# Moving the copies of a bias table from the GpSimd queue to the queue of the weight loads

## The chip, the cores and the metric

The kernel runs on one core of one Trainium2 chip. The metric is the device time of one execution in microseconds (us); lower is better. A core has TensorE (PE, with its weight loads PEld), VectorE (DVE), ScalarE (ACT), GpSimd (POOL) and SyncE (SP). SP computes nothing here: it issues DMAs. DMAs issued from SP, ACT and POOL are listed as separate queues, and the transfers of all queues are carried by the core's 16 DMA engines.

## The reference, cut to what matters

The reference is two transformer-like blocks for one sequence of 256 tokens with 1024 features, all in float32. The first block has two layers, each with a SwiGLU FFN, an attention and a second FFN, all modulated by a conditioning vector; the second block has convolutions, an attention to a memory and a feed-forward part with 16384 experts. The change concerns the attention of the first layer alone, a differential attention with a relative-position bias:

```python
def diff_attention(h, w_qkv, w_o, lam_params, subln_g, rel_bias, lambda_init):
    ...
    lf = lam_params.astype(jnp.float32)
    lam = jnp.exp(jnp.sum(lf[0] * lf[1])) - jnp.exp(jnp.sum(lf[2] * lf[3])) + lambda_init
    table = rel_bias.astype(jnp.float32)
    ...
        rel = q_pos[:, None] - k_pos[None, :]
        bias = jnp.take(table, t5_bucket(rel), axis=0)
        bias = jnp.transpose(bias, (2, 0, 1))[None, :, None]
        logits = jnp.einsum('bqhmd,bkhmd->bhmqk', qb, k).astype(jnp.float32) * scale + bias
        logits = jnp.where(rel >= 0, logits, -jnp.inf)
        p = jax.nn.softmax(logits, axis=-1)
        w = p[:, :, 0] - lam * p[:, :, 1]
        return jnp.einsum('bhqk,bkhe->bqhe', w.astype(v.dtype), v)
    ...
    o = rms_norm(o, subln_g) * (1 - lambda_init)
```

The bias depends on the head (8 of them) and on the distance of query and key alone, so for one head it is one line of values, shifted by one place from query to query.

## The kernel before, in words

Activations lie with features on the partitions: `xT` is 128 partitions x 8 x 256 tokens. Each float32 weight is split into a high and a low part, so that a product takes three matmuls (`mm3`, L147 to L149). Weights come through the class `Weights`: SP loads 1 MB into one of 3 `raw` buffers (L105); a raw tile has two pieces of 128x1024, and each is split by ACT (`whi`, L115) and DVE (`wlo`, L116) into one of 4 pairs of buffers, which TensorE reads. The modulation weights (`araw`, L355) go through SP too, as background work between the weight loads, and are reduced on DVE (L358).

The kernel begins with keys and values of the memory. Then comes `ffn(0, ...)`, the first FFN: 22 output tiles j of the hidden layer (one raw tile each, `ffn_in`), then 8 output tiles n of the projection back (`ffn_out`). For each n, `residual` updates `xT` on DVE, ACT squares the new tile (`sq`, L182, three buffers) and POOL adds the squares up (`sqa`, L193). The sum is multiplied with ones on TensorE (`po`, L177), and from that come the root mean square and the row of scales that the attention needs (`rstd`, L198 and L199; `along_row`, L215; `row`, L243). While the sum is made, TensorE runs the first pair of query tiles on the unscaled activations (`Norm.pair`); then `Norm.scale` writes the scaled `hi` and `lo` (L270 to L275), and the attention goes on. The second FFN ends in the same way, before the keys of the second layer.

The generator `prepare_bias` works beside the first FFN. Its first step loads a one-hot table, the bias table and the lambda parameters. The second multiplies them on TensorE to 8 lines of 384 values (8 partitions, one for each head; `mrow`) and writes these to DRAM (`line`). Then, for each pair of heads q, POOL copies the two lines 128 times to DRAM (`rows`, L515) and reads them back into `TB` (L517) with a step of 383, one less than a row, so that partition p gets its line shifted by p. The last two steps compute lambda (`ls`, L524; the exponent, L528; `nlam`, L529 and L530) and the scale `g08` (L526). The loop over j calls `next(beside)` at j = 4, 6, 8, 10, 12 and 14. `TB` is first read by the heads of the attention (L573).

`TB`, `nlam`, `g08` and the query tiles `qz` lie in the pool `tb`, whose space was used before by other tiles; `const` is a pool that lives from the beginning. The order of instructions on each engine is not that of the source: the framework's scheduler lays it out when the program is built, by its own estimate of when each instruction can start, and the instruction waits on the chip for what it needs. Each engine runs its own instructions in that order.

Of the kernel before, what the change touches and what calls it, by code (L numbers as in the profile page):

```python
# [10 lines left out]
F32 = mybir.dt.float32  # L11
# [42 lines left out]
def forward(ctx: ExitStack, tc: tile.TileContext, io, out, tap=None):  # L54
    nc = tc.nc
    pe, act, dve, pool, sync = nc.tensor, nc.scalar, nc.vector, nc.gpsimd, nc.sync

    const = ctx.enter_context(tc.tile_pool(name="const", bufs=1))
# [8 lines left out]
    def bank(tag, shape):  # L67
        return ps.tile(shape, F32, tag=tag, name=tag, bufs=BANKS[tag])

    def mm_bank(shape):  # L70
        return bank("mm", shape)

    def work(tag, shape, dt=F32, bufs=2, pool_=None):
        return (pool_ or wkp[0]).tile(shape, dt, tag=tag, name=tag, bufs=bufs)
# [13 lines left out]
    def v(name, i=0, n=1):  # L88
        c = VEC[name][0] + i
        return vec[:, c:c + n]  # L90
# [48 lines left out]
    def tick():  # L139
        rate[1] += rate[0]  # L140
        while rate[1] >= 1.0:
            rate[1] -= 1.0
            step()

    def mm3(o, a, b, start, stop):

        pe.matmul(o, a[0], b[0], start=start, stop=False)  # L147
        pe.matmul(o, a[0], b[1], start=False, stop=False)  # L148
        pe.matmul(o, a[1], b[0], start=False, stop=stop)  # L149
# [5 lines left out]
    def blk(piece, k, n=128):  # L155
        return piece[0][:, k * n:(k + 1) * n], piece[1][:, k * n:(k + 1) * n]

    def split_into(pair_hi, pair_lo, src, func=AF.Copy, **kw):

        act.activation(pair_hi, src, func, **kw)  # L160
        dve.tensor_tensor(pair_lo, src, pair_hi, op=ALU.subtract)  # L161
# [115 lines left out]
    def fm_pair(p0, p1, h):  # L277

        o = [mm_bank([128, T]), mm_bank([128, T])]
        for k in range(KT):  # L280
            for oo, pp in zip(o, (p0, p1)):
                mm3(oo, blk(pp, k), tok(h, k), k == 0, k == KT - 1)
        return o

    def fm_one(p, h, h32=None, n=T):
        o = mm_bank([128, n])
        for k in range(KT):
            if len(p) == 1:
                pe.matmul(o, p[0][:, k * 128:(k + 1) * 128], h32[:, k, :], start=(k == 0), stop=(k == KT - 1))  # L289
                continue  # L290
            mm3(o, blk(p, k), tok(h, k, 0, n), k == 0, k == KT - 1)
        return o
# [95 lines left out]
    def mod(name):  # L388
        while name not in mods:
            next(ada)  # L390
        return mods[name]
# [33 lines left out]
    def residual(n, o, s, st, norm):  # L425
        dve.scalar_tensor_tensor(xT[:, n, :], o, s, xT[:, n, :], op0=ALU.mult, op1=ALU.add)
        st.add(xT[:, n, :])
        norm.add(n)


    def ffn(f, norm, gate, following, more=None, done=False):

        with tc.tile_pool(name="ff", bufs=1) as fp:
            ghi = fp.tile([128, FKT, T], F32R, name="ghi")
            glo = fp.tile([128, FKT, T], F32R, name="glo")
            src = io[f"ffn_in{f}"]
            h = norm.h
            for j in range(FKT):
                if f == 0 and j in (4, 6, 8, 10, 12, 14):
                    next(beside)  # L440
                it = W.pieces(src[j])
                if j == 0 and not done:
                    og, ou = norm.pair(next(it), next(it))
                elif j < 2:
                    og, ou = fm_pair(next(it), next(it), h)
                else:
                    og = fm_one(next(it), h)
                    ou = fm_one(next(it), h)
                sg = work("sil", [128, T], bufs=2)
                act.activation(sg, og, AF.Silu)  # L450
                pr = work("pr", [128, T], bufs=2)
                dve.tensor_tensor(pr, sg, ou, op=ALU.mult)
                split_into(ghi[:, j, :], glo[:, j, :], pr)
                tick()
            tc.keep_in_program_order(act.preload_act_table(AF.Sqrt))
            s = mod(gate)
            st = Stat()
            nxt = following()
            src = io[f"ffn_out{f}"]

            def stream():
                for c in range(src.shape[0]):
                    for p in W.pieces(src[c]):
                        for k in range(8):
                            yield blk(p, k)
                    tick()

            wb = stream()
            for n in range(KT):
                o = mm_bank([128, T])  # L470
                for k in range(FKT):
                    mm3(o, next(wb), (ghi[:, k, :], glo[:, k, :]), k == 0, k == FKT - 1)
                residual(n, o, s[:, n:n + 1], st, nxt)
                if more is not None:
                    more.add(xT[:, n, :], scale=v("final_g", n))
        return st, nxt
# [8 lines left out]
    tbp = ask.enter_context(tc.tile_pool(name="tb", bufs=1))  # L485
    dram = ask.enter_context(tc.tile_pool(name="dr", bufs=1, space=bass.MemoryType.DRAM))
    TB = tbp.tile([128, 8, 256], F32, name="TB")
    nlam = tbp.tile([128, 1], F32, name="nlam")
    g08 = tbp.tile([128, 1], F32, name="g08")
    qz = [tbp.tile([128, 2, 256], F32, name=f"qz{i}") for i in range(4)]  # L490
    for t in qz:
        pool.memset(t[64:128, 0, :], 0.0)
# [2 lines left out]
    def prepare_bias():  # L495
        oh = tbp.tile([32, 384], F32, name="oh")
        rb = tbp.tile([32, 8], F32, name="rb")
        lamb = tbp.tile([128, 4, 64], F32, name="lamb")
        la = io["a_lambda"]
        pool.dma_start(out=oh, in_=io["t5"])  # L500
        pool.dma_start(out=rb, in_=io["rel_bias"])
        pool.dma_start(out=lamb, in_=bass.AP(tensor=la.tensor, offset=la.offset, ap=[[0, 128], [64, 4], [1, 64]]))
        mrow = tbp.tile([8, 384], F32, name="mrow")
        pool.memset(mrow[:, 0:256], 0.0)
        pool.memset(mrow[:, 256:384], BIG)
        yield
        pf = bank("lg", [8, 384])
        pe.matmul(pf, rb, oh, start=True, stop=True)
        dve.scalar_tensor_tensor(mrow, pf, -1.0, mrow, op0=ALU.mult, op1=ALU.add)
        line = dram.tile([8, 384], F32, name="line")  # L510
        pool.dma_start(out=line, in_=mrow)
        for q in range(4):
            yield
            rows = dram.tile([2, 128, 384], F32, name=f"rows{q}")
            pool.dma_start(out=rows, in_=line[2 * q:2 * q + 2, :].unsqueeze(1).to_broadcast([2, 128, 384]))  # L515

            pool.dma_start(out=TB[:, 2 * q:2 * q + 2, :],  # L517
                           in_=bass.AP(tensor=rows.tensor, offset=rows.offset + 127,
                                       ap=[[383, 128], [128 * 384, 2], [1, 256]]))
        yield  # L520
        lj = tbp.tile([128, 64], F32, name="lj")
        ls = tbp.tile([128, 2], F32, name="ls")
        for i in range(2):
            dve.tensor_tensor_reduce(out=lj, in0=lamb[:, 2 * i, :], in1=lamb[:, 2 * i + 1, :], scale=1.0,  # L524
                                     scalar=0.0, op0=ALU.mult, op1=ALU.add, accum_out=ls[:, i:i + 1])
        dve.tensor_scalar(g08, v("a_subln_g"), 1.0 - LAM0, None, op0=ALU.mult)  # L526
        yield
        act.activation(ls, ls, AF.Exp)  # L528
        dve.tensor_tensor(nlam, ls[:, 1:2], ls[:, 0:1], op=ALU.subtract)  # L529
        dve.tensor_scalar(nlam, nlam, -LAM0, None, op0=ALU.add)  # L530
        yield

    norm = norm_of("0_sc1", "0_sh1")
    norm.scale(r=st.rstd())
    beside = prepare_bias()
    next(beside)
    st, norm = ffn(0, norm, "0_gt1", lambda: norm_of("0_sc2", "0_sh2"), done=True)
    if tap:
        tap("x_ffn0", xT)
# [105 lines left out]

    rate[0] = 0.56
    st, norm = ffn(1, norm.scaled_by(st), "0_gt3", lambda: norm_of("k_sc1", "k_sh1"))
    rate[0] = 0.4
    if tap:
# [331 lines left out]
    with tc.tile_pool(name="pe0", bufs=1) as p0:  # L981
# [125 lines left out]
        with tc.tile_pool(name="pe1", bufs=1) as p1:  # L1107
# [90 lines left out]
            for t in range(2):  # L1198
# [13 lines left out]
                rows = out[t * 128:(t + 1) * 128]  # L1212
# [102 lines left out]
def program(arrays):  # L1315
    import concourse.bacc as bacc

    nc = bacc.Bacc("TRN2", target_bir_lowering=False, num_devices=1)
    io = {n: nc.dram_tensor(n, a.shape, mybir.dt.from_np(a.dtype), kind="ExternalInput").ap()
          for n, a in arrays.items()}  # L1320
    out = nc.dram_tensor("out", (T, D), F32, kind="ExternalOutput").ap()
    with tile.TileContext(nc) as tc:
        forward(tc, io, out)
    return nc
# [9 lines left out]
```

## Time and profile before

| | |
|---|---|
| median of 3 runs | 2270.47 us (2269.82 to 2273.29) |
| the profiled execution | 2270.32 us, its span 2268.5 us |
| TensorE busy | 98% of the span, mean granted clock 0.996 |
| VectorE, ScalarE, GpSimd busy | 77%, 55%, 4% |
| bytes moved by DMA | 467.76 MB, mean 206 GB/s |

A time such as 260 us is counted from the start of the span. The share of an engine is what it was busy of the span; "x" is followed by a number of instructions. In "A <- B: 7.8, 1, 7.8", the instruction A was held by B for 7.8 us in total, in one place, at most 7.8 us. [...]

### The profile page before, as it was taken

Reading aid. Unit: us, or ns where it says so; the run is one execution under the profiler, and the core shown is the slowest. Engines: PE = TensorE matmul, PEld = TensorE weight load, DVE = VectorE, ACT = ScalarE, POOL = GpSimd, SP = SyncE. Lnnn points to the kernel's source line nnn. Section 1 sums busy time; section 2 is a strip of 40 time slices with the busy share of each in tenths; the row PEclk is TensorE's granted clock in tenths of the full one; section 3 lists DMA queues with packets and bytes.
Section 4 is the critical chain, followed back from the end, with each engine's and each line's share of the span. In section 5 each row is a group of like instructions: output and inputs, shape, how many; then the busy total and the mean of one; then the engine's idle time right before and its main releaser. Section 6 shows DMA issues by size and latency. Waiting matters only on the chain.

```text
span 2268.5 us, 42687 instructions
## 1 busy us (share of the span) xinstructions
PE 2229.0 (98%) x16748; PEld 2131.5 (94%) x16748; DVE 1739.7 (77%) x3501; ACT 1258.6 (55%) x2389; POOL 85.3 (4%) x89
## 2 busy tenths in 40 slices
PE   8999899999999999999999999999999999999998
PEld 8999898999999999999999999999999999888887
DVE  7878667977777787765799886999668997666665
ACT  5544477544654457545523555445567776555555
POOL 0100000000100020000100010000000000000000
PEclk9999899999999999999999999999999999999999
DMA  9887644777668763555444453345543434555554
GB/s 364 297 325 300 231 168 164 301 275 293 245 263 300 292 231 129 216 182 182 164 159 165 161 219 115 117 184 186 186 155 144 145 136 152 193 192 188 185 187 157
DMA packets 68377, 467.76 MB, mean 206 GB/s; under 512 B 9888, under 2 KB 10184, under 8 KB 12368
## 3 DMA queue, kind: packets, MB, share of 16 engines
q1 hardware_dynamic: 64608, 461.67, 54.9%
q0 software_dynamic: 3280, 2.84, 0.5%
q8 instruction: 132, 2.16, 0.4%
q14 instruction: 69, 0.57, 0.1%
q10 hardware_dynamic: 288, 0.52, 0.1%
HBM read 463.88 MB, written 2.63 MB: 206 GB/s over the span
## 4 chain that ended last, share of the span: by engine, by line
PE 92%; DVE 3%; ACT 3%; issue 1%; POOL 0%; DMA 0%; ACTq 0%; DVEq 0%; POOLq 0%
PE mm L149 22%; PE mm L147 22%; PE mm L148 22%; PE mm L1171 8%; PE lg L1171 8%; PE lg L1126 2%; PE mm L289 2%; PE po L177 1%; ACT whi L115 1%; DVE wlo L116 1%; DVE lo L238 0%; DVE lo L275 0%; DVE nt L270 0%; PE po L962 0%; ACT e L576 0%
## 5 line engine op out<-in xcount | busy, mean ns | idle before, releaser
L115 ACT ACTIVATE whi<-raw 128x1024 fp32r<-128x1024 f32 x696 | 733.9, 1059 | 624.2 <-PE mm L148 414.6
L116 DVE TENSOR_TENSOR wlo<-raw,whi 128x1024 fp32r<-128x1024 f32 x696 | 850.5, 1226 | 295.8 <-ACT whi L115 291.0
L147 PE MATMUL mm<-hi,whi 128*128 128x256 f32 x3144 | 900.2, 287 | 2.6 <-ACT hi L274 2.1
L149 PE MATMUL mm<-hi,wlo 128*128 128x256 f32 x3144 | 892.7, 284 | 1.3 <-DVE wlo L116 1.2
L148 PE MATMUL mm<-lo,whi 128*128 128x256 f32 x3144 | 887.2, 282 | 0.1
L147 PEld LDWEIGHTS mm<-hi,whi 128*128 128x128 f32 x3144 | 595.2, 190 | 5.0 <-ACT hi L274 2.6
L149 PEld LDWEIGHTS mm<-hi,wlo 128*128 128x128 f32 x3144 | 596.4, 190 | 3.0 <-DVE wlo L116 2.7
L148 PEld LDWEIGHTS mm<-lo,whi 128*128 128x128 f32 x3144 | 596.9, 190 | 1.8 <-DVE wlo L116 0.6
L149 PE MATMUL mm<-ghi,wlo 128*128 128x256 f32 x704 | 197.4, 280 | 0.0
L147 PE MATMUL mm<-ghi,whi 128*128 128x256 f32 x704 | 197.4, 280 | 0.0
L148 PE MATMUL mm<-glo,whi 128*128 128x256 f32 x704 | 197.4, 280 | 0.0
L358 DVE CUSTOM_DVE_ANT_0 araw<-araw,cb 128x1024 f32<-128x1024 f32 x160 | 191.4, 1225 | 1.0 <-ACT cb L407 1.0
L160 ACT ACTIVATE vph<-S 128x128 fp32r<-128x128 f32 x256 | 77.1, 302 | 131.9 <-PE lg L1171 131.8
L148 PEld LDWEIGHTS mm<-glo,whi 128*128 128x128 f32 x704 | 132.7, 188 | 0.0
L147 PEld LDWEIGHTS mm<-ghi,whi 128*128 128x128 f32 x704 | 132.7, 188 | 0.0
L149 PEld LDWEIGHTS mm<-ghi,wlo 128*128 128x128 f32 x704 | 132.7, 188 | 0.0
L161 DVE TENSOR_TENSOR vpl<-S,vph 128x128 fp32r<-128x128 f32 x256 | 73.4, 288 | 44.3 <-PE lg L1171 43.8
L824 DVE SCALAR_TENSOR_TENSOR cfc<-cf,vec,cfc 128x256 f32<-128x256 f32 x240 | 100.0, 490 | 0.0
L1118 DVE TENSOR_SCALAR ohA<-cst,sel 128x128 f32<-128x128 f32 x256 | 82.2, 342 | 21.8 <-PE lg L1126 20.8
L1171 PE MATMUL mm<-whi,vph 128*128 128x512 f32 x256 | 80.7, 395 | 0.2 <-ACT vph L160 0.2
L1171 PE MATMUL mm<-wlo,vph 128*128 128x512 f32 x256 | 80.9, 395 | 0.0
L1171 PE MATMUL lg<-whi,vpl 128*128 128x512 f32 x256 | 80.8, 395 | 0.0
(392 smaller groups left out, 3277.7 us busy)
## 6 DMA issues: line engine op xcount, KB each, us to landing
raw<-ffn_in SPq DMA_DIRECT2D x88, 1024.0 KB, 4.9
araw<-ada SPq DMA_DIRECT2D x72, 1024.0 KB, 6.9
raw<-peer_u SPq DMA_DIRECT2D x64, 1024.0 KB, 4.8
raw<-peer_v SPq DMA_DIRECT2D x64, 1024.0 KB, 4.8
raw<-ffn_out SPq DMA_DIRECT2D x44, 1024.0 KB, 4.8
araw<-kv_ada SPq DMA_DIRECT2D x8, 1024.0 KB, 6.8
raw<-w_cf SPq DMA_DIRECT2D x8, 1024.0 KB, 4.7
raw<-w_scx SPq DMA_DIRECT2D x8, 1024.0 KB, 4.8
```

Of the source, the lines that this page charges most:

```text
L115: act.activation(hi[:, :m], r, AF.Copy)
L116: last_split[0] = dve.tensor_tensor(lo[:, :m], r, hi[:, :m], op=ALU.subtract)
L147: pe.matmul(o, a[0], b[0], start=start, stop=False)
L148: pe.matmul(o, a[0], b[1], start=False, stop=False)
L149: pe.matmul(o, a[1], b[0], start=False, stop=stop)
L160: act.activation(pair_hi, src, func, **kw)
L161: dve.tensor_tensor(pair_lo, src, pair_hi, op=ALU.subtract)
L289: pe.matmul(o, p[0][:, k * 128:(k + 1) * 128], h32[:, k, :], start=(k == 0), stop=(k == KT - 1))
L358: dve.tensor_tensor_reduce(out=raw[:, i, :], in0=raw[:, i, :], in1=cb, scale=1.0, scalar=0.0, op0=ALU.mult, op1=ALU.add, accum_out=acc[:, ...
L824: dve.scalar_tensor_tensor(o, cf[:, i, j:j + T], w, o, op0=ALU.mult, op1=ALU.add)
L1118: dve.tensor_scalar(A, iota, sel3[:, 0, t:t + 1], sel3[:, 2, t:t + 1], op0=ALU.is_equal, op1=ALU.mult)
L1171: pe.matmul(acc[t][d], lh, rh[:, d * 512:(d + 1) * 512], start=s0, stop=s1)
```

## The change

The copies and read-backs of the bias table are issued by SP, the queue of the weight loads, and no longer by POOL. The DRAM tile `line` is gone: each of the 8 lines is copied from its own partition of `mrow`, 128 times, straight to `rows`, so there are two copies for each pair of heads where there was one. All copies are issued first, one pair of heads a step, and then the four read-backs, one a step. The steps stand at each j from 3 to 12 (ten steps), where they stood at six even j from 4 to 14. `nlam` and `g08` are allocated in the pool `const`.

```diff
             for j in range(FKT):
-                if f == 0 and j in (4, 6, 8, 10, 12, 14):
+                if f == 0 and 3 <= j <= 12:
                     next(beside)
...
-    nlam = tbp.tile([128, 1], F32, name="nlam")
-    g08 = tbp.tile([128, 1], F32, name="g08")
+    nlam = const.tile([128, 1], F32, name="nlam")
+    g08 = const.tile([128, 1], F32, name="g08")
...
         dve.scalar_tensor_tensor(mrow, pf, -1.0, mrow, op0=ALU.mult, op1=ALU.add)
-        line = dram.tile([8, 384], F32, name="line")
-        pool.dma_start(out=line, in_=mrow)
+        copies = []
         for q in range(4):
             yield
             rows = dram.tile([2, 128, 384], F32, name=f"rows{q}")
-            pool.dma_start(out=rows, in_=line[2 * q:2 * q + 2, :].unsqueeze(1).to_broadcast([2, 128, 384]))
-
-            pool.dma_start(out=TB[:, 2 * q:2 * q + 2, :],
+            copies.append(rows)
+            for i in range(2):
+                hd = 2 * q + i
+                sync.dma_start(out=rows[i:i + 1], in_=mrow[hd:hd + 1, :].unsqueeze(1).to_broadcast([1, 128, 384]))
+        for q, rows in enumerate(copies):
+            yield
+
+            sync.dma_start(out=TB[:, 2 * q:2 * q + 2, :],
                            in_=bass.AP(tensor=rows.tensor, offset=rows.offset + 127,
                                        ap=[[383, 128], [128 * 384, 2], [1, 256]]))
         yield
```

## Rows read from the trace of the kernel before

**Rows 1.** The page: busy time by engine, and the chain by engine.
```profile
PE 2229.0 (98%) x16748; PEld 2131.5 (94%) x16748; DVE 1739.7 (77%) x3501; ACT 1258.6 (55%) x2389; POOL 85.3 (4%) x89
...
PE 92%; DVE 3%; ACT 3%; issue 1%; POOL 0%; DMA 0%; ACTq 0%; DVEq 0%; POOLq 0%
```
**Rows 2.** Windows; the columns are named in the first line.
```profile
core 0: us, PE busy (x) PEld busy (x) DVE busy (x) ACT busy (x) POOL busy (x), PEclk, DMA share, GB/s
60.00:70.00 10.00, 9.17 (x70) 8.38 (x68) 6.43 (x17) 5.39 (x10) 2.52 (x9) 1.00 0.51 215
70.00:80.00 10.00, 9.48 (x57) 8.41 (x58) 9.57 (x16) 5.45 (x9) 2.08 (x5) 0.83 0.77 239
150.00:160.00 10.00, 10.00 (x86) 10.00 (x85) 7.12 (x11) 5.27 (x8) 0.00 (x0) 1.00 0.84 316
260.00:300.00 40.00, 29.68 (x214) 28.33 (x213) 24.75 (x43) 18.29 (x35) 5.47 (x4) 0.83 0.39 152
585.00:625.00 40.00, 38.58 (x319) 37.13 (x317) 29.85 (x54) 26.56 (x46) 7.04 (x2) 1.00 0.64 241
```
**Rows 3.** Waits from 260 to 290 us: total us, times, longest.
```profile
POOL sqa L193 <- ACT sq L182: 44.1, 1, 44.1
...
PE po L177 <- POOL sqa L193: 7.8, 1, 7.8
```
**Rows 4.** Timeline of ACT, ends of the first and second FFN: start, duration.
```profile
222.66 0.42 ACT L182 ACTIVATE sq<-xT 128x256 f32<-128x256 f32 x1 [0.21 <-DVE xT L426]
...
265.96 2.00 ACT L115 ACTIVATE whi<-raw 128x1024 fp32r<-128x1024 f32 x2 [3.92 <-issue]
267.87 1.01 ACT L182 ACTIVATE sq<-xT 128x256 f32<-128x256 f32 x3
...
582.92 0.42 ACT L182 ACTIVATE sq<-xT 128x256 f32<-128x256 f32 x1 [0.30 <-DVE xT L426]
...
591.08 0.40 ACT L182 ACTIVATE sq<-xT 128x256 f32<-128x256 f32 x1
```
**Rows 5.** Timeline of POOL in the first FFN.
```profile
125.23 1.09 POOL L515 DMA_DIRECT2D rows<-line  x1
140.24 0.75 POOL L517 DMA_DIRECT2D TB<-rows  x1 [13.92 <-DMA rows<-line]
215.73 1.20 POOL L193 TENSOR_TENSOR sqa<-sq 128x256 f32<-128x256 f32 x1 [74.74 <-ACT sq L182]
216.88 0.74 POOL L517 DMA_DIRECT2D TB<-rows  x1
...
268.42 5.70 POOL L193 TENSOR_TENSOR sqa<-sqa,sq 128x256 f32<-128x256 f32 x4 [44.06 <-ACT sq L182]
```
**Rows 6.** DMA, 85 to 200 us: queues with packets, MB, share; issues with landing.
```profile
q1 hardware_dynamic: 4750, 34.59, 80.2%
q0 software_dynamic: 3088, 2.40, 7.2%
...
rows<-line POOLq DMA_DIRECT2D x4, 384.0 KB, 26.6
TB<-rows POOLq DMA_DIRECT2D x3, 256.0 KB, 14.2
```
**Rows 7.** SP issues kA<-FT (16 KB, one partition written), and a window around it.
```profile
625.75 0.62 SPq L698 DMA_DIRECT2D kA<-FT  x1
...
626.90:627.30 0.40, 0.40 (x5) 0.40 (x4) 0.00 (x0) 0.40 (x3) 0.00 (x0) 1.00 0.17 41
```
**Rows 8.** A raw load on SP, its splits, and landings of raw, 85 to 180 us.
```profile
120.88 0.33 SPq L105 DMA_DIRECT2D raw<-ffn_in  x1
...
132.89 1.06 ACT L115 ACTIVATE whi<-raw 128x1024 fp32r<-128x1024 f32 x1 [1.50 <-issue]
...
135.77 1.06 ACT L115 ACTIVATE whi<-raw 128x1024 fp32r<-128x1024 f32 x1 [1.55 <-PE mm L148]
...
134.88 1.22 DVE L116 TENSOR_TENSOR wlo<-raw,whi 128x1024 fp32r<-128x1024 f32 x1
...
DMA to landing us min/median/max: 4.7/8.1/10.8
```
**Rows 9.** Timeline of DVE: the first use of the table.
```profile
300.26 0.29 DVE L573 CUSTOM_DVE_ANT_0 e<-lg,TB 128x128 f32<-128x128 f32 x1 [0.35 <-PE lg L570]
```
**Rows 10.** Timelines of DVE and ACT around the write of g08.
```profile
67.15 0.16 DVE L526 TENSOR_SCALAR g<-vec 128x1 f32<-128x1 f32 x1 [2.64 <-PE mm L149]
68.06 0.88 DVE L275 SCALAR_TENSOR_TENSOR lo<-nt,mod_sh,hi 128x256 fp32r<-128x256 f32 x2 [0.75 <-ACT hi L274]
...
66.79 0.84 ACT L323 ACTIVATE xa_v<-mm,rstd 128x256 f32<-128x256 f32 x2 [3.68 <-PE mm L149]
```

## The prediction

> **What bounds the kernel now.** I read four views in this order: the page's busy shares and chain, windows around the end of the first FFN beside the end of the second, the waits and the order on ACT and POOL there, and the DMA view of the first FFN.
>
> TensorE bounds the whole: busy 98% of the span, 92% of the chain that ended last [rows 1]. The steps of the change lie in the first FFN and act on the attention that follows it. Inside the FFN TensorE never waits: 10.00 of 10 us, 86 matmuls [rows 2]. So an edit there can only cost, unless it reaches a place where TensorE stands.
>
> There is one such place. At the end of the first FFN, 260 to 300 us, TensorE is busy 29.68 of 40 us and runs 214 matmuls at a mean granted clock of 0.83; the same passage at the end of the second FFN, 585 to 625 us, has 38.58 us, 319 matmuls and clock 1.00 [rows 2]. The longest TensorE wait there is the row statistic's matmul for `sqa` on POOL, 7.8 us; POOL in turn had waited 44.1 us for a square from ACT [rows 3]. The order on ACT says why: the third square runs at 222.66, then the next three come in one block at 267.87, behind two weight splits at 265.96. At the end of the second FFN each square stands beside its own tile (582.92, 591.08) [rows 4]. A square needs one of three buffers, so the fourth waits until POOL has added the first two. On POOL the bias DMAs share that stretch: the read-back of table part 2 at 140.24, the first addition at 215.73, the read-back of part 3 only at 216.88, the last four additions together at 268.42 [rows 5]. The copy that part 3 needs was issued at 125.23 [rows 5] and landings of such copies take 26.6 us [rows 6], so it had been in DRAM since about 152. That it stands behind an addition of 215 us shows an order laid out for a far slower bias chain on POOL. I read the late squares as the consequence: when the order was made, POOL was taken up by DMAs, the additions were late, and the squares lost their buffers.
>
> **The change, part by part.** The base is the profiled execution, 2270.32 us: 1.8 us beside its span of 2268.5 and 0.15 under the median of 2270.47.
>
> *POOL is freed.* One `line` write, four copies and four read-backs leave POOL. If the squares then fall in beside their tiles, this passage costs what the second FFN's does. By matmuls: 40 us at 86 per 10 us are 344; 130 are missing here, 25 there; 105 at 0.116 us are 12.2 us. [...] I take 12.2 us. Above: all 130, 15.1 us. Below: nothing, if the order stays.
>
> *The copies.* Eight copies of 128 rows x 1536 B (196.6 KB) go on SP's queue, each from one partition. Before, a pair was one DMA from a DRAM line. Their data has to pass the same 16 engines, now in one queue with the weight loads, so what counts is how long a copy holds that queue. No row shows a read from a single partition. From below: POOL's queue moved 2.40 MB, copies included, in 7.2% of 115 us [rows 6], 8.3 us of all engines, so 0.7 us a copy. From above: half of a 26.6 us landing, 13.3 us a copy. The nearest row is a transfer of 16.4 KB into one partition: the stretch 626.90 to 627.30 holds it whole, at 0.17 of the engines and 41 GB/s [rows 7]. By its engine time (0.068 us for 16.4 KB) a copy costs 0.8 us, by its elapsed time at most 4.8 us. I take the geometric middle, 2.0 us: 16 us for eight.
>
> What covers it: a raw load issued at 120.88 is split at 132.89, 12.0 us later [rows 8]: the fifth split after it, since two tiles of two pieces lie ahead. A split waits for one of four buffers, so three pieces of 2.88 us lie ahead of TensorE, 8.6 us, less 1.06 and 1.22 us for the split itself [rows 8]: 6.3 us more. Landing takes 4.7 us at least [rows 8], which leaves 13.6 us; loads that landed in 10.8 us stopped nothing. The SP queue fills 80.2% of the engines [rows 6], so four tiles of 5.75 us have 4.6 us to spare. Cover: 18.2 us, or 2.3 us a copy. My 16 us fit; a weight load would be next to be late, then the splits, then TensorE. Cost: 0.
>
> *The read-backs.* Four of 256 KB: by the engine time above about 0.9 us each; their former landing was 14.2 us [rows 6]. SP must wait for the copies four steps earlier, with weight loads queued behind it and TensorE waiting for those. If a step really stands at its output tile, four tiles (23 us) pass in between and there is no wait; if the steps move together, SP holds for one landing under load, 8.1 to 10.8 us [rows 8], inside the 13.6. The bias is first used at 300.26 [rows 9], so the table has over 100 us. Cost: 0. Twelve DMA issues at 0.33 us are 4 us of a queue that mostly waits [rows 8].
>
> *Steps one tile earlier.* The small matmul, its VectorE evacuation and the lambda exponent stay the same instructions. The exponent's two table loads on ScalarE are 2.6 us, covered by a TensorE that is busy throughout; that is my bound for either sign.
>
> *Lambda out of the pool.* VectorE's write of `g08` waits 2.64 us for TensorE, in a pool whose space was in use. But the next VectorE instruction then waits 0.75 us for ScalarE, which itself was held by an earlier evacuation until 66.79 [rows 10]. So the end of this stall goes to ScalarE: gain 0. At most it reorders the start of the FFN: 45 matmuls short of 172 in 60 to 80 us [rows 2], 5.2 us.
>
> Sum: 2270.3 - 12.2 = 2258.1. Own range 2252 (all of 15.1 and part of the 5.2) to 2266.
>
> [...] The kA transfer moved 16.4 KB in 0.4 us [rows 7], at least 41 GB/s on one partition. [...]
>
> **The rivals.**
>
> *A single partition feeds slowly.* A copy takes 4.8 to 8 us and holds the weight queue. For it: 16.4 KB are a twelfth of a copy, and a copy is 128 reads of one row; copies from one DRAM line landed only after 26.6 us. Against: the 41 GB/s. At 6.4 us eight take 51.2 us, less 18.2 of cover: TensorE stands 33 us, in the first FFN. 2258 + 33 = 2291; at 4.8 us 2278, at 8 us 2304, at 13.3 us 2346. It decides against the change from 3.8 us a copy, where (8 x 3.8 - 18.2) eats the 12.2. [...]
>
> *Around that point.* At 3.2 to 4.4 us a copy gain and stall cancel: 2266 to 2275.
>
> *The change doesn't do what frees the passage.* The squares stay late since the order has another cause, for instance that the splits of the value projection were simply ready first. For it: these splits do stand ahead of the squares [rows 4]. Against: the second FFN has the same splits and no such block. With hidden copies: 2270.
>
> **How the numbers follow.** Forecast 0.42: the order on POOL speaks plainly, the copy price is the nearest row's. Slow partition 0.36: its price has no row against it of the same kind. Cancelling 0.09. Order unchanged 0.13, of which 0.11 near 2270 and 0.02 faster through lambda. A measurement of this kernel tells 0.2% (4.5 us) from no change. Faster: 0.42 + 0.02 = 0.44. Same: 0.09 + 0.11 = 0.20. Slower: 0.36. Forecast 2258; the range must reach into the slow case: 2251 to 2303 leaves out copies above 7.9 us (about 0.12) and a little below (0.05).
>
> **What would show it.** Right: squares beside their tiles near 207 to 262, additions on POOL one by one, no wait of `po` for `sqa`, clock 1.00 in 260 to 300, about 320 matmuls there, and raw loads in the FFN landing under 13 us. Wrong: TensorE waiting for splits and splits for raw loads between 85 and 180, with raw landings of 20 us and more (slow partition); or the three squares in a block again after the pair (order unchanged); or SP waiting long for `rows` at the read-backs. The weakest step is the 2.0 us a copy.

## The result and the profile after

The changed kernel takes 2292.02 us (median of 4 runs, 2290.52 to 2293.17) against 2271.38 us for the kernel before on the same chip: ratio 1.009, 95% interval 1.0073 to 1.0108. It is 20.6 us slower, where 12.2 us faster was forecast; the time lies inside the range, at the price of the rival "a single partition feeds slowly". The profiled execution has a span of 2291.4 us.

The page after, busy times and the chain by engine, to be read beside [rows 1]:

```profile
PE 2232.0 (97%) x16748; PEld 2138.6 (93%) x16748; DVE 1740.8 (76%) x3501; ACT 1259.8 (55%) x2389; POOL 76.2 (3%) x80
...
PE 90%; DVE 3%; ACT 3%; DMA 2%; issue 1%; POOL 0%; ACTq 0%; DVEq 0%; POOLq 0%; SPq 0%
```

POOL has nine instructions fewer. New in the chain is DMA with 2%, and the page's chain by line puts 2% to `raw<-ffn_in`: in the changed kernel weight loads set the end for a while. The windows after, in the columns of [rows 2], show where:

```profile
80.00:90.00 10.00, 10.00 (x83) 10.00 (x84) 9.06 (x19) 8.19 (x12) 0.00 (x0) 1.00 0.79 137
90.00:100.00 10.00, 10.00 (x86) 10.00 (x85) 3.52 (x7) 2.15 (x5) 0.00 (x0) 1.00 0.86 29
100.00:110.00 10.00, 0.58 (x5) 0.38 (x4) 0.85 (x2) 0.42 (x1) 0.00 (x0) 0.64 0.86 27
110.00:120.00 10.00, 2.54 (x10) 2.25 (x11) 2.72 (x3) 2.00 (x2) 0.00 (x0) 0.50 0.94 231
120.00:130.00 10.00, 6.17 (x40) 5.96 (x39) 2.78 (x6) 0.80 (x2) 0.00 (x0) 0.84 0.89 87
130.00:140.00 10.00, 5.97 (x26) 5.68 (x27) 4.99 (x8) 2.01 (x2) 0.00 (x0) 0.50 0.94 205
140.00:150.00 10.00, 4.26 (x28) 3.76 (x28) 2.31 (x4) 2.80 (x4) 0.00 (x0) 0.84 0.95 313
...
260.00:300.00 40.00, 40.00 (x341) 40.00 (x340) 30.43 (x38) 18.74 (x24) 5.09 (x5) 1.00 0.71 266
```

The last two columns of the second and third line are the finding: the 16 DMA engines are busy 86% of the time and move 27 to 29 GB/s, where the first FFN before has 316 GB/s at a share of 0.84 [rows 2]. The busy share alone does not say how much data flows. TensorE lives on its buffers until 100 us and then stands, and while it stands its granted clock, the share of full speed at which it was allowed to run, falls to 0.50 (110 to 120 us). The last line is the other half of the story: the passage that had 214 matmuls in 40 us [rows 2] has 341 at clock 1.00. (This FFN ends later than before, so the stretch does not hold the same work; that the end of the FFN itself runs full is shown by the next line of the window, 300 to 340 us with 39.98 us busy and 322 matmuls, and by the squares further down.)

The DMA view after, 84 to 112 us: packets and mean rate, then the queue with packets, MB and share:

```profile
DMA packets 550, 0.80 MB, mean 28 GB/s; under 512 B 50, under 2 KB 547, under 8 KB 547
...
q1 hardware_dynamic: 549, 0.78, 85.7%
```

In 28 us 0.78 MB pass, in packets nearly all of them under 2 KB: four copies of 128 rows. That is 7.0 us a copy for these four (196.6 KB at 28 GB/s). The waits after, 95 to 155 us, and the chain of the stretch (start, us):

```profile
PE mm L147 <- ACT whi L115: 30.5, 6, 16.7
...
ACT whi L115 <- DMA raw<-ffn_in: 24.9, 4, 14.6
```

```profile
96.05 20.12 DMA raw<-ffn_in
116.24 31.13 DMA raw<-ffn_in
```

TensorE waits for splits, the splits for raw loads, and two raw loads take 20 and 31 us of the chain. The prediction had named this as the mark of the slow partition. SP's own timeline says how the loads got behind the copies:

```profile
82.99 12.96 SPq L517 DMA_DIRECT2D rows<-mrow  x4
96.05 7.12 SPq L105 DMA_DIRECT2D raw<-ffn_in  x1
103.21 7.17 SPq L355 DMA_DIRECT2D araw<-ada  x1
110.43 1.99 SPq L517 DMA_DIRECT2D rows<-mrow  x2
...
118.65 8.83 SPq L521 DMA_DIRECT2D TB<-rows  x1
```

Four copies were issued in one block, so "one pair of heads a step" in the source did not become one pair a tile on SP. Behind the copies the issue of one DMA took 7.12, 7.17 and 8.83 us, where it was 0.33 us [rows 8].

The squares after, on ACT, and their additions on POOL (timelines), for [rows 4] and [rows 5]:

```profile
246.06 0.42 ACT L182 ACTIVATE sq<-xT 128x256 f32<-128x256 f32 x1 [1.69 <-DVE xT L426]
...
269.99 0.42 ACT L182 ACTIVATE sq<-xT 128x256 f32<-128x256 f32 x1
...
277.28 0.42 ACT L182 ACTIVATE sq<-xT 128x256 f32<-128x256 f32 x1 [1.69 <-DVE xT L426]
...
285.88 0.42 ACT L182 ACTIVATE sq<-xT 128x256 f32<-128x256 f32 x1 [1.75 <-DVE xT L426]
```

```profile
270.55 1.07 POOL L193 TENSOR_TENSOR sqa<-sqa,sq 128x256 f32<-128x256 f32 x1 [7.21 <-ACT sq L182]
277.85 0.73 POOL L193 TENSOR_TENSOR sqa<-sqa,sq 128x256 f32<-128x256 f32 x1 [6.23 <-ACT sq L182]
```

The block of three squares is gone, each stands beside its tile, and POOL adds them one by one. From the first square to the first use of the table it is 79.6 us (246.06 to 325.7), where it was 92.9 (207.34 to 300.26, [rows 9]): the forecast gain is there, 13.3 us, and is outweighed, because the first square itself comes 38.7 us later.

### The profile page after: what moved, and what is told of

It reads as the page before. It is cut to its first block, busy times and chain, and to the rows that moved or that the text cites. A ratio compares the mean times of both kernels' runs of the same rounds, so it can differ in the third digit from the quotient of the medians.

```text
span 2291.4 us, 42688 instructions
## 1 busy us (share of the span) xinstructions
PE 2232.0 (97%) x16748; PEld 2138.6 (93%) x16748; DVE 1740.8 (76%) x3501; ACT 1259.8 (55%) x2389; POOL 76.2 (3%) x80
## 4 chain that ended last, share of the span: by engine, by line
PE 90%; DVE 3%; ACT 3%; DMA 2%; issue 1%; POOL 0%; ACTq 0%; DVEq 0%; POOLq 0%; SPq 0%
PE mm L149 22%; PE mm L147 22%; PE mm L148 22%; PE mm L1175 8%; PE lg L1175 8%; PE lg L1130 2%; PE mm L289 2%; DMA raw<-ffn_in 2%; PE po L177 1%; ACT whi L115 1%; DVE wlo L116 1%; DVE lo L275 0%; DVE lo L238 0%; DVE nt L270 0%; ACT e L580 0%
## 5 line engine op out<-in xcount | busy, mean ns | idle before, releaser
L115 ACT ACTIVATE whi<-raw 128x1024 fp32r<-128x1024 f32 x696 | 733.0, 1058 | 605.6 <-PE mm L148 401.7
L147 PE MATMUL mm<-hi,whi 128*128 128x256 f32 x3144 | 904.1, 288 | 31.1 <-ACT whi L115 30.5
L147 PEld LDWEIGHTS mm<-hi,whi 128*128 128x128 f32 x3144 | 598.4, 191 | 34.3 <-ACT whi L115 32.0
L147 PE MATMUL mm<-ghi,whi 128*128 128x256 f32 x704 | 197.7, 281 | 0.0
L147 PEld LDWEIGHTS mm<-ghi,whi 128*128 128x128 f32 x704 | 132.8, 189 | 0.0
L161 DVE TENSOR_TENSOR vpl<-S,vph 128x128 fp32r<-128x128 f32 x256 | 73.8, 290 | 37.8 <-PE lg L1175 37.6
L1175 PE MATMUL lg<-whi,vph 128*128 128x512 f32 x256 | 80.3, 393 | 0.0
```

Source lines behind the costliest of these rows:

```text
L115: act.activation(hi[:, :m], r, AF.Copy)
L1175: pe.matmul(acc[t][d], lh, rh[:, d * 512:(d + 1) * 512], start=s0, stop=s1)
```

## The experiments

The theory after the result: a copy from one partition takes 7.0 us, at 28 GB/s, with the DMA engines 86% busy meanwhile, and neighbouring partitions share that rate (the author's hypothesis, which no trace had shown and e5 and e6 put to the test); freeing POOL gains some 12 us; a further 4 us come from somewhere after 1425 us. The rivals are named at each run. All times are medians beside runs of the kernel before on the same chip (2270.6 to 2271.2 us).

| run | lines copied from, by | time, us | ratio, 95% interval |
|---|---|---|---|
| e1 | a DRAM line, SP | 2262.47 | 0.9952 to 0.9979 |
| e2 | partitions, SP, 4 copies | 2270.95 | 0.9992 to 1.0011 |
| e3 | as before; statistic on TensorE | 2269.14 | 0.9984 to 1.0003 |
| e4 | as before; lambda in `const` | 2267.08 | 0.9975 to 0.9993 |
| e5 | partitions 0 to 7, SP, one DMA | 2277.69 | 1.0017 to 1.0039 |
| e6 | partitions 0, 4 ... 28, SP, one DMA | 2258.32 | 0.9930 to 0.9960 |
| e7 | as before; two unused `const` tiles | 2267.44 | 0.9974 to 0.9992 |
| e8 | a DRAM line, POOL, one DMA; lambda in `const` | 2254.15 | 0.9912 to 0.9939 |
| e9 | partitions, POOL | 2309.27 | 1.0145 to 1.0179 |
| e10 | partitions, ACT | 2284.33 | 1.0044 to 1.0078 |
| e11 | as changed; lambda in `tb` | 2295.54 | 1.0087 to 1.0121 |
| e12 | as before; one unused tile in the last stage | 2264.81 | 0.9967 to 0.9985 |

**The partition taken away (e1).** The changed kernel, the lines written to DRAM once and copied from there:

```diff
+        line = dram.tile([8, 384], F32, name="line")
+        sync.dma_start(out=line, in_=mrow)
...
-                sync.dma_start(out=rows[i:i + 1], in_=mrow[hd:hd + 1, :].unsqueeze(1).to_broadcast([1, 128, 384]))
+                sync.dma_start(out=rows[i:i + 1], in_=line[hd:hd + 1, :].unsqueeze(1).to_broadcast([1, 128, 384]))
```

> The changed kernel, but the lines go to a DRAM tile first and the eight copies read that tile; queue, steps, read-backs and lambda stay. Theory (one partition feeds a copy slowly, and the weight loads stand behind it in SP's queue): no long copy is left, the TensorE stall of the first FFN is gone and the gain at its end stays, 2258 us (2253 to 2266). Rival A (twelve more DMAs and their waits on SP are the cost, whatever they read): 2280 to 2295. Rival B (128 writes of a repeated line to DRAM are the cost): 2280 to 2295.

2262.47 us: 29.6 us less than the changed kernel, with the same eight copies on the same queue. The order on SP is thus not what costs most; the source of the copies is. A smaller stall stays, and the waits of SP in e1, 95 to 140 us, point to a cause:

```profile
SPq L105 <- DVE wlo L116: 21.5, 5, 10.5
SPq L355 <- DVE acc_gt L358: 12.5, 1, 12.5
```

A modulation load (L355) waited 12.5 us for VectorE in SP's order, and weight loads stood behind it; in the kernel before no such wait of SP is longer than 5.7 us from 85 to 140 us. That this wait makes the rest of the stall was not tried by itself.

**The cost halved (e2).** Only four lines are copied, two steps fewer are taken, and the heads 4 to 7 use the rows of heads 0 to 3, so this kernel computes another bias. All else is as in the changed kernel.

```diff
-                if f == 0 and 3 <= j <= 12:
+                if f == 0 and 3 <= j <= 12 and j not in (6, 7):
...
-        for q in range(4):
+        for q in range(2):
...
-        for q, rows in enumerate(copies):
+        for q, rows in enumerate(copies + copies):
```

> The changed kernel with the lines of four heads copied instead of eight; the table of heads 4 to 7 is read back from the lines of heads 0 to 3, so that part of the bias is another one. Four read-backs stay. Theory: 4 x 7 us = 28 us of copies, of which the buffers of weights cover about 20, so a stall of 5 to 10 us and 2262 to 2270 us. Rival A (waits of SP at the read-backs): nearly as slow as with eight copies, 2285. Rival C (the loss is in proportion to the copies, with no cover): 2275.

2270.95 us, 21.1 us less than with eight. Half the copies give back 21 of 38 us of stall (38 is worked out below, from e8). That lies just above the theory's 2262 to 2270 and under the 2275 of rival C, which has no cover. By the first square, read at e8 below, half the copies leave half of the delay, as rival C has it.

**One part by another way (e3).** The kernel before, with the statistic of the first FFN summed on TensorE, so that no addition on POOL is waited for:

```diff
-            st = Stat()
+            st = Stat(on_pe=(f == 0))
```

> The kernel before, its DMAs on GpSimd as they were; only the sums of squares of the first FFN are made on TensorE instead of GpSimd. Theory (the squares came late since their buffers hung on additions that were laid out behind the DMAs of GpSimd): the squares fall in beside their tiles and the 12 us at the end of the first FFN come back, less some 3 us for 12 more small matmuls: 2262 us (2258 to 2265). Rival (the late squares have another cause): 2271 to 2275.

2269.14 us: no difference that can be measured. The squares do fall in beside their tiles (206.80 to 266.64), with POOL's eight bias DMAs in place, which ties the block of squares to the additions on POOL. The passage is full (49.79 of 50 us busy, 250 to 300 us), but at the end of the attention TensorE then stands more (34.50 of 40 us busy, 340 to 380 us, where it was 37.44 with 284 matmuls in the kernel before):

```profile
250.00:300.00 50.00, 49.79 (x399) 47.97 (x398) 39.84 (x85) 32.32 (x64) 0.00 (x0) 1.00 0.61 232
...
340.00:380.00 40.00, 34.50 (x226) 30.14 (x225) 23.70 (x86) 28.46 (x82) 0.00 (x0) 0.87 0.34 132
```

The first use of the table comes at 291.4 us, 8.9 us earlier than before, but by the last rstd (L198) only 1.5 us of it are left (1422.6 against 1424.2). The order behind the passage is another one here, so this run could not say what the passage alone is worth. e8 could.

**Lambda alone (e4), and put back (e11).** The kernel before with `nlam` and `g08` in `const`; the changed kernel with them in `tb` (the diff of e4 reversed):

```diff
-    nlam = tbp.tile([128, 1], F32, name="nlam")
-    g08 = tbp.tile([128, 1], F32, name="g08")
+    nlam = const.tile([128, 1], F32, name="nlam")
+    g08 = const.tile([128, 1], F32, name="g08")
```

> The kernel before with lambda and its scale in the long-lived pool, nothing else. Theory (the 2.6 us wait of VectorE only passes on to ScalarE): 2271 us, within 2 us of before. Rival (that wait held the start of the first FFN): 2266 to 2269.

> The changed kernel with nlam and g08 back in the pool tb, all else as changed. Theory (the two parts add up; the const tiles are worth 4 us in the last stage and nothing else): 2296, 844 us from the last rstd to the end of the span. Rival (the 4 us of the last stage come with any change of the kernel): 2292, 840 us.

2267.08 and 2295.54 us: the two tiles are worth 3.6 us either way, so the parts of the change add up. But the gain is not at `g08`. The last rstd (L198) starts at 1424.2 us in the kernel before and at 1425.6 in e4; from there to the end of the span are 844.3 and 840.3 us.

**Where those 4 us come from (e7, e12).** The kernel before, once with two unused tiles in `const`, once with one unused tile of 64 bytes in the last stage's own pool; lambda untouched in both:

```diff
+    pads = [const.tile([128, 1], F32, name=f"pad{i}") for i in range(2)]
+    for p_ in pads:
+        dve.memset(p_, 0.0)
```

```diff
             S1 = p1.tile([128, NI - MID, T], F32, name="S1")
+            pad = p1.tile([128, 16], F32, name="pad")
+            dve.memset(pad, 0.0)
```

> The kernel before, with two unused tiles of 128x1 allocated in the pool const (and set to zero once by VectorE); nlam and g08 stay where they were. Theory (the 4 us that appear in the last stage whenever nlam and g08 lie in const come from what their allocation does to the addresses of the tiles after them, not from lambda): time 2267, and from the last rstd to the end of the span 840 us instead of 844. Rival (they come from the freed wait of g08 or from lambda's own instructions): 2271, 844 us.

> The kernel before with one unused tile of 64 bytes a partition in the last stage's own pool, ahead of the split scores vph and vpl (set to zero once by VectorE); const, nlam and g08 stay as they were. In the kernel before vph and vpl begin at byte addresses of remainder 96 by 128, as the split weights do; here, as in the changed kernel and in the run with two unused const tiles, they begin 64 bytes further, at remainder 32, and no tile outside this pool moves. Theory (the 4 us hang on where vph and vpl lie, alone): about 1313 matmuls instead of 1293 from 1950 to 2250 us, time 2267. Rival (they hang on another tile that the const tiles moved, xT and the rest): 1293, time 2271.

2267.44 and 2264.81 us: the gain is there without any change to lambda, and also when only the last stage's pool moves. The window from 1950 to 2250 us, first of the kernel before, then of e12:

```profile
1950.00:2250.00 300.00, 300.00 (x1293) 243.25 (x1292) 185.32 (x323) 168.53 (x324) 0.00 (x0) 1.00 0.53 189
```

```profile
1950.00:2250.00 300.00, 300.00 (x1312) 246.43 (x1311) 187.83 (x328) 171.57 (x329) 0.00 (x0) 1.00 0.53 190
```

TensorE is busy throughout in both and does 1293 or 1312 matmuls; the changed kernel does 1313. Grouped by form, such a matmul of L1171 lasts 395 ns on the mean in the kernel before and 390 to 393 ns in the others. What moved in e12 are the tiles of that pool behind the unused one, by 64 bytes a partition, and of these the matmuls read the split scores `vph` and `vpl`; why this makes the matmuls 1.5% denser no run tells. e12 lies 2.6 us under e7 at the same rate of matmuls; that difference is not explained.

**Partition or group of partitions (e5, e6).** All eight lines in one DMA on SP's queue, from partitions 0 to 7, and from partitions 0, 4, 8 to 28:

```diff
-                sync.dma_start(out=rows[i:i + 1], in_=mrow[hd:hd + 1, :].unsqueeze(1).to_broadcast([1, 128, 384]))
+        rows = dram.tile([8, 128, 384], F32, name="rows")
+        sync.dma_start(out=rows, in_=mrow[0:8:1, :].unsqueeze(1).to_broadcast([8, 128, 384]))
```

In e6 `mrow` has 32 partitions and the copy reads `mrow[0:32:4, :]`. In both, the small product is taken from a copy of the bias table (in e6 padded with zero columns, which puts each line on its partition), and three empty steps stand in for the steps of the other copies.

> The changed kernel, with its eight copies put into one DMA on SP's queue that reads partitions 0 to 7, all eight lines at once. Theory (what limits a copy is the path of a group of neighbouring partitions: 0 to 3 and 4 to 7, some 28 GB/s each): the 1.57 MB take 28 us; the stall of 36 us in the first FFN falls to about 10 or 15, time about 2265 to 2270. Rival A (each partition by itself gives 28 GB/s): 7 us, no stall but that of the run with the DRAM line, 2262 or below. Rival B (28 GB/s is all that such a broadcast read from SBUF gives, wherever it reads, or the rows of the DMA are walked line after line): 56 us as in the changed kernel, 2290 to 2295.

> As the run on two groups, but the eight lines lie on partitions 0, 4, 8 to 28 (the small product is taken with a bias table padded with zero columns), so that no two share a group of four neighbours. Theory (limit by group of partitions): about 7 to 10 us for all copies, time 2255 to 2263. Rival A (limit by partition): the same as on partitions 0 to 7, within 2 us. Rival B (28 GB/s wherever it reads, or line after line): 2290 to 2295.

2277.69 and 2258.32 us. The two DMAs differ in nothing but the partitions that they read, and 19.4 us lie between them: it matters which eight partitions are read, so the limit is not one of each partition by itself (rival A wanted the same time), nor of a broadcast read as such (rival B wanted 2290 and more). The DMA view shows the rates directly while nearly all packets are those of the copies, first of e5 (84 to 94 us), then of e6 (84 to 86 us):

```profile
DMA packets 289, 0.50 MB, mean 50 GB/s; under 512 B 3, under 2 KB 281, under 8 KB 281
```

```profile
DMA packets 260, 0.41 MB, mean 207 GB/s; under 512 B 0, under 2 KB 259, under 8 KB 259
```

So it is some 28 GB/s in the changed kernel's copies of one partition each, 50 from eight neighbouring partitions and 207 from eight that lie four apart; as 50 and 207 lie above 28, the lines of these DMAs were read side by side. Two groups of four neighbours in e5 and eight groups in e6 fit these rates, at 25 and 26 GB/s a group (50 / 2, 207 / 8); that the groups are of four is an estimate from these three rates, and no run tried another spacing. e5 is still some 8 us above what was expected of it, and why is open: its engines are only 40% busy in that stretch, yet the weight load behind the copies waits. The issue of that load on SP takes long too, in e5 and then in e6:

```profile
83.89 0.84 SPq L515 DMA_DIRECT2D rows<-mrow  x1
84.83 8.80 SPq L105 DMA_DIRECT2D raw<-ffn_in  x1
```

```profile
82.06 0.84 SPq L515 DMA_DIRECT2D rows<-mrow  x1
83.00 2.42 SPq L105 DMA_DIRECT2D raw<-ffn_in  x1
```

TensorE's longest wait for a split (L147 for L115, 90 to 165 us) is 20.8 us in e5 and 2.0 us in e6: four partitions apart, the eight lines passed without a long stall.

**POOL's chain cut short (e8).** The kernel before, lambda in `const`, and one copy and one read-back for all eight heads in place of four each, still on POOL's queue:

```diff
-        for q in range(4):
-            yield
-            rows = dram.tile([2, 128, 384], F32, name=f"rows{q}")
-            pool.dma_start(out=rows, in_=line[2 * q:2 * q + 2, :].unsqueeze(1).to_broadcast([2, 128, 384]))
...
+        rows = dram.tile([8, 128, 384], F32, name="rows")
+        pool.dma_start(out=rows, in_=line.unsqueeze(1).to_broadcast([8, 128, 384]))
+        yield
+        pool.dma_start(out=TB, in_=bass.AP(tensor=rows.tensor, offset=rows.offset + 127,
+                                           ap=[[383, 128], [128 * 384, 8], [1, 256]]))
```

> The kernel before with nlam and g08 in const and with POOL's bias chain cut short: line as before, then one copy DMA for all eight heads and one read-back DMA, all on POOL's queue; SP's queue is left alone. Theory (the squares came late since POOL's chain of eight DMAs was laid out slowly; no copy holds up weight loads): the passage at 260 to 300 us runs full, -8 to -12 us there, and -4 us in the last stage: 2255 to 2260. Rival (the gain there is given back in the attention, as in the run with the statistic on TensorE): 2265 to 2268.

2254.15 us, the best of all: 17.0 us under the kernel before (ratio 0.9926, 0.9912 to 0.9939) and 37.9 under the changed one. Its windows, 100 to 120 us and the end of the first FFN, and POOL's timeline:

```profile
100.00:110.00 10.00, 10.00 (x86) 10.00 (x85) 9.02 (x16) 4.23 (x7) 0.00 (x0) 1.00 0.93 366
110.00:120.00 10.00, 10.00 (x85) 10.00 (x85) 7.41 (x11) 5.23 (x8) 0.93 (x1) 1.00 0.98 369
...
260.00:300.00 40.00, 39.98 (x322) 38.91 (x321) 31.77 (x75) 29.28 (x67) 0.00 (x0) 1.00 0.54 206
```

```profile
89.64 1.12 POOL L514 DMA_DIRECT2D rows<-line  x1 [5.24 <-DMA line<-mrow]
113.19 0.93 POOL L516 DMA_DIRECT2D TB<-rows  x1 [22.44 <-DMA rows<-line]
215.82 1.20 POOL L193 TENSOR_TENSOR sqa<-sq 128x256 f32<-128x256 f32 x1 [101.70 <-ACT sq L182]
223.50 1.13 POOL L193 TENSOR_TENSOR sqa<-sqa,sq 128x256 f32<-128x256 f32 x1 [6.48 <-ACT sq L182]
```

No stall in the copies, none at the end of the FFN. The table is first used at 287.0 us instead of 300.26 [rows 9], 13.3 us earlier, and the last stage gives the 4 us. e8 thus has both gains and no stall, and serves as the floor: what a run lies above 2254.2 us is its stall. That is 37.9 us for the changed kernel, 23.5 for e5, 16.8 for e2, 8.3 for e1, 4.2 for e6. The start of the first square (ACT L182) measures the stall by the traces alone, without the later stages:

```profile
207.35 0.42 ACT L182 ACTIVATE sq<-xT 128x256 f32<-128x256 f32 x1 [1.69 <-DVE xT L426]
```

Against these 207.35 us of e8 it comes 38.7 us later in the changed kernel (246.06), 23.8 in e5, 19.3 in e2, 8.7 in e1 and 2.1 in e6. The two ways differ by up to 2.5 us.

**Another queue (e9, e10).** The changed kernel's eight copies issued by POOL, or by ACT:

```diff
-                sync.dma_start(out=rows[i:i + 1], in_=mrow[hd:hd + 1, :].unsqueeze(1).to_broadcast([1, 128, 384]))
+                pool.dma_start(out=rows[i:i + 1], in_=mrow[hd:hd + 1, :].unsqueeze(1).to_broadcast([1, 128, 384]))
```

> The changed kernel with its eight copies from the partitions of mrow issued by POOL; the read-backs stay on SP. The third to sixth squares stand late in this order, as in the kernel before, so there is no gain at the end of the first FFN: what is read is the first FFN from 80 to 160 us. Theory A (a copy stops the weight loads because it stands ahead of them in SP's queue): raw loads land under 13 us, TensorE is full from 80 to 160 us, time about 2267. Theory B (a copy's rows hold the 16 DMA engines, whatever queue it came from): raw loads land at 15 us and more while the copies run, and TensorE loses 20 to 36 us there, time 2285 to 2303.

> The changed kernel with its eight copies issued by ACT; the squares stand beside their tiles in this order. Theory A (only the order in SP's queue costs): no stall from 80 to 160 us, 2255 to 2259, and issues on ACT take a third of a us each. Theory B (the engines are held): TensorE loses 20 to 36 us in the first FFN, 2275 to 2292. A third way: an issue on ACT takes up to 7 us when its queue is full, as it did on SP, and then ACT's splits are late by that, which its timeline would show.

2309.27 and 2284.33 us: theory A (2267 and 2255 to 2259) falls. In e9 no copy stands in SP's queue, and the weight loads are stopped all the same: raw loads took up to 53.6 us to land, the DMA engines were over 90% busy from 100 to 130 us at 31 to 86 GB/s, and TensorE did nothing for 30 us. Theory B fits these numbers, but its loss of 20 to 36 us was too small. The copies had been issued in 4.13 us, all at once. The windows of e9, with the end of its first FFN:

```profile
90.00:100.00 10.00, 10.00 (x86) 10.00 (x85) 6.18 (x10) 4.00 (x7) 0.00 (x0) 1.00 1.01 67
100.00:110.00 10.00, 3.80 (x32) 3.60 (x31) 2.38 (x4) 0.00 (x0) 0.00 (x0) 0.83 0.96 31
...
110.00:140.00 30.00, 0.00 (x0) 0.00 (x0) 0.00 (x0) 0.00 (x0) 0.00 (x0) 0.50 0.91 111
...
300.00:340.00 40.00, 29.68 (x214) 28.36 (x213) 24.28 (x41) 17.84 (x33) 5.47 (x4) 0.83 0.43 165
```

The last line also speaks on the other question: with eight DMAs on POOL the bubble of [rows 2] is back, to the digit (29.68 us, 214 matmuls, clock 0.83), some 40 us later. It, and not a longer stall, is most of what sets e9 apart from the changed kernel: the first square comes at 248.06 us, 40.7 us after that of e8, against 38.7.

In e10 ACT issued the copies one by one between its splits, at about 0.5 us each, so the third way in its stated form (a long issue) falls; the stall is spread, 30.2 us above the floor by time and 29.4 by the first square. But ACT was held otherwise, as the waits from 75 to 165 us show:

```profile
ACT ghi L160 <- DMA TB<-rows: 11.8, 2, 8.1
```

By the profile, ACT stood in both places until a read-back had landed and then issued the next copy (115.99 and 131.68 us). So e10 does not say how much of its stall is the engines and how much is ACT, nor whether pacing the copies helps; e9 is the run that decides against theory A.

## Why the prediction was wrong

The step that failed is "I take the geometric middle, 2.0 us" a copy. It put eight copies at 16 us, inside the cover of 18.2, and so their cost at 0. A copy was 7.0 us. The middle was taken between 0.8 and 4.8 us, both from one row, and 7.0 lies above both: "at most 4.8 us" was no bound. That row, 16.4 KB in 0.4 us [rows 7], is a write into one partition of a twelfth of a copy, and does not show what a partition gives over 200 KB. The wider bounds, 0.7 and 13.3 us, held the true value, and the rival's 4.8 to 8 us too; of these 4.8 comes from [rows 7], while no row or run shows the 8, and the runs showed 7.0.

With 7.0 us in the prediction's own sum the stall is 8 x 7.0 - 18.2 = 37.8 us; measured it is 37.9 against e8 and 38.7 by the first square. That the two agree so closely is partly luck. The cover of 18.2 us is not a constant: for the four copies of e2 the same sum gives 9.8, and 16.8 to 19.3 were measured, about half of the stall for half of the copies; and e1 has 8.3 us of stall without any slow copy. A block of copies issued at once may leave no room for loads between them; no run separates this.

**POOL is freed, -12.2.** Right, and a little small: e8 gains 17.0, of which 3.6 (e4) are lambda's tiles, so 13.4 us, under the bound of 15.1; the changed kernel's own trace has 13.3. The reason is shown as well: fewer DMAs on POOL put the squares beside their tiles (changed kernel, e8), eight copies on POOL put them back in a block (e9), and without the additions on POOL they stand beside their tiles although the DMAs are there (e3).

**Read-backs, 0.** Not separated. One of them took 8.83 us to issue on SP behind the copies, which "if a step really stands at its output tile" had left out. In e1, where the four stand on SP as well, they landed in 7.2 us (median) and the whole stall was 8.3 us; how much of that is theirs is open.

**Steps one tile earlier, 0.** Not tried by itself; it is part of what e1 has with those 8.3 us.

**Lambda, 0.** Right where it was looked for: after the change VectorE waits 3.55 us for ScalarE at L275, as foreseen, and the first table use of e4 is no earlier. Wrong in the sum: -3.6 us in the last stage (e4, e7, e11, e12), through the place of other tiles. Nothing in the rows of before pointed there.

The parts add up from the traces, to 1.2 us: 2271.4 us before, 38.7 for the late first square, 13.3 less from there to the first use of the table, 3.6 less in the last stage (e4) make 2293.2, against 2292.02 measured.

## What to carry to other kernels

The price of these transfers out of SBUF went by which partitions they read as well as by their bytes (28 GB/s from one partition a copy, 50 from eight neighbours, 207 from eight that lie four apart), and a short burst did not show that: where the trace has no row of the same kind and size, a middle of far bounds is no forecast, and the point from which the price decides (here 3.8 us a copy) deserves the first look. DMA share and GB/s are to be read together: engines that were 86% busy at 28 GB/s let hardly a weight load pass, and putting the copies on POOL's queue (e9) did not help. A chain of small DMAs on an idle engine cost 13 us here through the order of work that is laid out around it; merging them (e8) kept the good of the change without its cost.

## What was not expected of the hardware

- Behind copies from single partitions in its queue, SP spent 7.12, 7.17 and 8.83 us on the issue of a single DMA, where it was 0.33 us [rows 8], and in e9, with the copies on POOL's queue, two weight loads took 28.49 us to issue; on ACT the copies of e10, spread out, took about 0.5 us each to issue.
- An unused tile of 64 bytes a partition in the last stage's pool, which shifts the split scores that the matmuls read, changed their rate from 1293 to 1312 in 300 us at the same granted clock of 1.00.
- Copies from one partition on POOL's queue stopped weight loads on SP's as long as the same copies on SP's own queue did (first square 40.7 and 38.7 us late), in e9 with 30 us without a matmul.
